# GpSimd in place of SyncE as the issuer of four loads and the first store in a one-core elementwise kernel

## The chip, the cores and the metric

The kernel runs on one core of a Trainium2 chip. The metric is the device time of one execution in microseconds; the median of three runs before the change is 119.82 us (119.6 to 119.83).

The core has several engines, each with its own queue of instructions. Here VectorE (DVE) multiplies, ScalarE (ACT) applies the activation, and SyncE (SP), ACT and GpSimd (POOL) may issue DMA transfers between HBM and the on-chip memory SBUF, which has 128 partitions. The transfers themselves are carried out by 16 DMA engines. TensorE (PE) does nothing in this kernel. Engines wait for each other through semaphores.

## The reference

Both inputs are float32 arrays of 1024 x 4096 elements, 16.8 MB each, and so is the output.

```python
z = x * y
return 0.5 * z * (1 + np.tanh(np.sqrt(2 / np.pi) * (z + 0.044715 * z ** 3)))
```

It is the product of x and y, put through the tanh form of GELU. Each element is read once from x and once from y, and written once: 33.55 MB in and 16.78 MB out.

## The kernel before, in words

The arrays are taken as flat and divided into three pieces, `PIECES`. Spread over 128 partitions, a piece has 1,280, 16,384 or 15,104 float32 columns; a row of it, the part of one partition, is contiguous in HBM and has 5,120, 65,536 or 60,416 bytes. I call them the small, the big and the last piece.

All of x has its place in SBUF (`xs`, 32,768 columns). The product and the activation overwrite it, and the stores read from there. For y there is only a buffer of 20,440 columns (`ys`), so the later y pieces reuse columns of the first one; `Y_LOADS` gives the order of the y pieces (big, last, small) and where each goes, and `Y_FREE` how many multiplications must be done before a load may overwrite.

The order of everything is written out by hand, with raw semaphores:

- `_hoist` puts two loads at the very start of the program: the small x piece on SP, and the big x piece on ACT.
- SP then waits for the small x piece, and issues the first y piece (big; `load_y`, L75) and the last x piece (`load_x`, L71). It waits until three multiplications are done and issues the second y piece (last), then until four are done and issues the third y piece (small).
- DVE multiplies (L99) in steps: four of 4,096 columns for the big piece, seven of 2,048 and one of 768 for the last piece, one of 1,280 for the small one. Each step raises `sem_mul`. Ahead of each piece DVE waits for its x and y.
- ACT applies GELU (L107) to the same columns after each multiplication and raises `sem_act`.
- SP issues the three stores, in the order big, last, small (L116), each when the activations of its piece are done (L115, L116). The first of them waits as well for `sem_y[-2]`, the landing of the second y piece. SP then waits for the first two stores (L118), clears the semaphores (L121) and waits for the last store (L122).

So five of the transfers that SP issues in the middle (four loads and the first store) stand in one queue with the stores that come after. The lines of the first store's waits are these:

```python
for i, (a, b) in enumerate(STORES):
    if i == 0:
        nc.sync.wait_ge(sem_y[-2], 16)
    nc.sync.wait_ge(sem_act, done[b])
```

Of the kernel before, what the change touches and what calls it, by code (L numbers as in the profile page):

```python
# [1 line left out]

# [4 lines left out]


F32 = mybir.dt.float32
GELU = mybir.ActivationFunctionType.Gelu_apprx_tanh  # L10

PIECES = [(0, 1280), (1280, 17664), (17664, 32768)]

Y_LOADS = [(1280, 17664, 4056), (17664, 32768, 0), (0, 1280, 15104)]

Y_FREE = [0, 3, 4]

STEPS = [[4096] * 4, [2048] * 7 + [768], [1280]]  # L20
STORES = [(1280, 17664), (17664, 32768), (0, 1280)]
Y_BUF = 20440


def _hoist(nc, issued):

    here = nc.cur_bb.bb.instructions
    first = nc.main_func.blocks[0].instructions
    for ins in issued:
        del here[next(k for k, i in enumerate(here) if i is ins or i.name == ins.name)]  # L30
    engine = issued[0].engine
    at = next(
        k
        for k, i in enumerate(first)
        if i.engine == engine and type(i).__name__ == "InstDrain"
    )
    first[at:at] = issued


@with_exitstack  # L40
def kernel(
    ctx: ExitStack,
    tc: tile.TileContext,
    x: bass.AP,
    y: bass.AP,
    out: bass.AP,
):
    nc = tc.nc
    P = nc.NUM_PARTITIONS

    def columns(t, a, b):

        flat = t.flatten_outer_dims().rearrange("r c -> (r c)")
        pa, pb = next(q for q in PIECES if q[0] <= a and b <= q[1])
        return flat[P * pa : P * pb].rearrange("(p c) -> p c", p=P)[:, a - pa : b - pa]


    tc.close()
    tc.compile()

    xs = nc.alloc_sbuf_tensor("xs", [P, PIECES[-1][1]], F32).ap()
    ys = nc.alloc_sbuf_tensor("ys", [P, Y_BUF], F32).ap()
    sem_x = [nc.alloc_semaphore(f"sem_x{i}") for i in range(len(PIECES))]
    sem_y = [nc.alloc_semaphore(f"sem_y{i}") for i in range(len(Y_LOADS))]
    sem_mul = nc.alloc_semaphore("sem_mul")
    sem_act = nc.alloc_semaphore("sem_act")
    sem_o = [nc.alloc_semaphore(f"sem_o{i}") for i in range(len(STORES))]

    def load_x(i, engine=nc.sync):
        a, b = PIECES[i]  # L70
        return engine.dma_start(out=xs[:, a:b], in_=columns(x, a, b)).then_inc(sem_x[i], 16)  # L71

    def load_y(i):
        a, b, r = Y_LOADS[i]
        return nc.sync.dma_start(  # L75
            out=ys[:, r : r + b - a], in_=columns(y, a, b)
        ).then_inc(sem_y[i], 16)

    _hoist(nc, [load_x(0).ins])
    _hoist(nc, [load_x(1, nc.scalar).ins])  # L80
    nc.sync.wait_ge(sem_x[0], 16)
    load_y(0)
    load_x(2)
    for i in range(1, len(Y_LOADS)):
        if Y_FREE[i]:
            nc.sync.wait_ge(sem_mul, Y_FREE[i])
        load_y(i)

    nc.scalar.wait_ge(sem_x[0], 16)
    n = 0  # L90
    done = {}
    for i, (a, b, r) in enumerate(Y_LOADS):
        for j, (xa, xb) in enumerate(PIECES):
            if xa <= a < xb:
                nc.vector.wait_ge(sem_x[j], 16)
        nc.vector.wait_ge(sem_y[i], 16)  # L96
        c = a
        for w in STEPS[i]:
            nc.vector.tensor_mul(  # L99
                out=xs[:, c : c + w],  # L100
                in0=xs[:, c : c + w],
                in1=ys[:, r + c - a : r + c - a + w],
            ).then_inc(sem_mul, 1)
            n += 1
            done[c + w] = n
            nc.scalar.wait_ge(sem_mul, n)
            nc.scalar.activation(  # L107
                out=xs[:, c : c + w], in_=xs[:, c : c + w], func=GELU
            ).then_inc(sem_act, 1)
            c += w  # L110

    for i, (a, b) in enumerate(STORES):
        if i == 0:
            nc.sync.wait_ge(sem_y[-2], 16)
        nc.sync.wait_ge(sem_act, done[b])  # L115
        nc.sync.dma_start(out=columns(out, a, b), in_=xs[:, a:b]).then_inc(sem_o[i], 16)  # L116
    for i in range(len(STORES) - 1):
        nc.sync.wait_ge(sem_o[i], 16)  # L118
    nums = sorted(s.num for s in [*sem_x, *sem_y, *sem_o[:-1], sem_mul, sem_act])
    assert nums == list(range(nums[0], nums[-1] + 1))  # L120
    nc.sync.sem_clear(range(nums[0], nums[-1] + 1))  # L121
    nc.sync.wait_ge(sem_o[-1], 16).then_inc(sem_o[-1], -16)  # L122


# [1 line left out]
_INS = ['x', 'y']  # L126
_OUTS = [((1024, 4096), 'float32')]


# [23 lines left out]
```

## Time and profile before

| | |
|---|---|
| median of the runs | 119.82 us (119.6 to 119.83) |
| span of the profiled execution, first to last instruction | 118.5 us |
| median less span: what lies around the instructions | 1.3 us |
| DVE busy | 35.2 us in 13 multiplications |
| ACT busy | 30.9 us, of it 29.6 in 13 activations |
| GpSimd busy | 0.2 us, four memsets at the start |
| moved by DMA | 50.33 MB, 425 GB/s on average over the span |
| DMA issues | 8 on SP, 1 on ACT |

The DMA issues of the profiled execution, with their times from the trace (issue to landing):

| transfer | issued by, at | landed after |
|---|---|---|
| small x, 640 KB | SP, 0.00 us | 13.6 us |
| big x, 8192 KB | ACT, 0.12 us | 30.4 us |
| first y (big) | SP, 13.57 us | 29.0 us |
| last x, 7552 KB | SP, 13.96 us | 46.5 us |
| second y (last) | SP, 55.79 us | 22.5 us |
| third y (small) | SP, 60.12 us | 19.7 us |
| first store (big) | SP, 78.27 us | 20.9 us |
| second store (last) | SP, 96.55 us | 20.4 us |
| third store (small) | SP, 97.71 us | 20.8 us |

A view of the page has one line per group or per queue. In the row of the DMA engines, each digit is the busy share of one fortieth of the span in tenths, over 16 engines. In the list of DMA queues the columns are packets, megabytes, and the share of 16 engines' span that the packets took. In the list of waits they are the total in microseconds, how often, and the longest. In the table of stretches they are the length, the busy time of DVE, ACT and GpSimd with the number of instructions, the granted TensorE clock, the DMA share and GB/s. "SPq" is SP's queue of instructions; q1 is the DMA queue that SP feeds, and q10 the one that ACT feeds.

### The profile page before, as it was taken

How to read it: one execution, taken by the hardware profiler on the slowest of the kernel's cores; microseconds unless marked ns; L12 is line 12 of the kernel's file. 1: busy time of each engine (PE TensorE's matmuls, PEld its weight loads, DVE VectorE, ACT ScalarE, POOL GpSimd, SP SyncE). 2: the span in 40 equal slices, each digit the busy share in tenths (PEclk: the TensorE clock that was granted, in tenths of full speed). 3: DMA queues.
4: the chain of work that ended last, by engine and by line, in shares of the span. 5: the costliest groups of instructions: out<-in, count | busy, mean ns of one | idle time of the engine just before them, and what ended most of it. 6: DMA issues, size and time to landing. Idle time of an engine off the chain costs nothing.

```text
span 118.5 us, 83 instructions
## 1 busy us (share of the span) xinstructions
DVE 35.2 (30%) x13; ACT 30.9 (26%) x14; POOL 0.2 (0%) x4
## 2 busy tenths in 40 slices
DVE  0000000000000069999920000059999940000000
ACT  0000000000000000999975000006998990000000
POOL 0000000000000000000000000000000000000000
DMA  9888899889988897798797797798899887977975
GB/s 492 382 382 382 354 597 464 354 354 465 597 354 354 354 632 347 326 632 347 326 632 347 326 632 347 326 575 354 354 531 531 354 354 326 653 326 326 653 326 221
DMA packets 1296, 50.33 MB, mean 425 GB/s; under 512 B 144, under 2 KB 144, under 8 KB 528
## 3 DMA queue, kind: packets, MB, share of 16 engines
q1 hardware_dynamic: 1152, 41.94, 82.3%
q10 hardware_dynamic: 144, 8.39, 16.5%
HBM read 33.55 MB, written 16.78 MB: 425 GB/s over the span
## 4 chain that ended last, share of the span: by engine, by line
DMA 55%; DVE 24%; ACT 3%; issue 1%; DVEq 0%
DMA ys<-in_y_dram 43%; DVE xs L99 24%; DMA xs<-in_x_dram 11%; ACT xs L107 3%; DVEq L96 0%
## 5 line engine op out<-in xcount | busy, mean ns | idle before, releaser
L99 DVE TENSOR_TENSOR xs<-xs,ys 128x2048 f32<-128x2048 f32 (+3 forms) x13 | 35.2, 2778 | 60.9 <-DMA ys<-in_y_dram 60.9
L107 ACT ACTIVATE xs<-xs 128x2048 f32<-128x2048 f32 (+3 forms) x13 | 29.6, 2300 | 19.6 <-DVE xs L99 19.6
L107 ACT ACT_TABLE_LOAD x1 | 1.3, 1283 | 47.2 <-DVE xs L99 47.2
L137 POOL MEMSET const-uint8-127<- 128x1 uint8 x1 | 0.1, 102 | 0.0
L137 POOL MEMSET const-bfloat16-1.0<- 128x1 bf16 x1 | 0.1, 101 | 0.0
L137 POOL MEMSET const-float32-0.0<- 128x1 f32 x1 | 0.1, 98 | 0.2 <-issue 0.2
L137 POOL MEMSET const-float32-1.0<- 128x1 f32 x1 | 0.1, 98 | 0.0
## 6 DMA issues: line engine op xcount, KB each, us to landing
xs<-in_x_dram SPq DMA_DIRECT2D x1, 7552.0 KB, 46.5
ys<-in_y_dram SPq DMA_DIRECT2D x1, 7552.0 KB, 22.5
out_dram<-xs SPq DMA_DIRECT2D x1, 7552.0 KB, 20.4
xs<-in_x_dram SPq DMA_DIRECT2D x1, 640.0 KB, 13.6
ys<-in_y_dram SPq DMA_DIRECT2D x1, 640.0 KB, 19.7
out_dram<-xs SPq DMA_DIRECT2D x1, 640.0 KB, 20.8
xs<-in_x_dram ACTq DMA_DIRECT2D x1, 30.4
ys<-in_y_dram SPq DMA_DIRECT2D x1, 29.0
```

Source lines behind the costliest of these rows:

```text
L99: nc.vector.tensor_mul(out=xs[:, c : c + w], in0=xs[:, c : c + w], in1=ys[:, r + c - a : r + c - a + w],).then_inc(sem_mul, 1)
L107: nc.scalar.activation(out=xs[:, c : c + w], in_=xs[:, c : c + w], func=GELU).then_inc(sem_act, 1)
L137: nc = _bacc.Bacc("TRN2", target_bir_lowering=False, num_devices=1)
```

## The change

GpSimd takes over the five transfers in the middle: the waits and the issues of all three y pieces, of the last x piece and of the first store. SP keeps the small x piece at the start, the second and third store and the waits at the end; ACT keeps the big x piece. The first store's wait for the second y piece is removed, and it waits for its activations alone. In GpSimd's queue the five stand in the order in which SP had them, after the memsets of the start.

```diff
     def load_y(i):
         a, b, r = Y_LOADS[i]
-        return nc.sync.dma_start(
+        return nc.gpsimd.dma_start(
             out=ys[:, r : r + b - a], in_=columns(y, a, b)
         ).then_inc(sem_y[i], 16)
 
     _hoist(nc, [load_x(0).ins])
     _hoist(nc, [load_x(1, nc.scalar).ins])
-    nc.sync.wait_ge(sem_x[0], 16)
+    nc.gpsimd.wait_ge(sem_x[0], 16)
     load_y(0)
-    load_x(2)
+    load_x(2, nc.gpsimd)
     for i in range(1, len(Y_LOADS)):
         if Y_FREE[i]:
-            nc.sync.wait_ge(sem_mul, Y_FREE[i])
+            nc.gpsimd.wait_ge(sem_mul, Y_FREE[i])
         load_y(i)
...
     for i, (a, b) in enumerate(STORES):
-        if i == 0:
-            nc.sync.wait_ge(sem_y[-2], 16)
-        nc.sync.wait_ge(sem_act, done[b])
-        nc.sync.dma_start(out=columns(out, a, b), in_=xs[:, a:b]).then_inc(sem_o[i], 16)
+        engine = nc.gpsimd if i == 0 else nc.sync
+        engine.wait_ge(sem_act, done[b])
+        engine.dma_start(out=columns(out, a, b), in_=xs[:, a:b]).then_inc(sem_o[i], 16)
```

## The prediction

> **What bounds the kernel now.** I read the page's DMA parts first, then the chain that ended last, the stretches of the span, the waits of SP's queue, and last the trace's records of single DMA packets.
>
> ```profile
> DMA  9888899889988897798797797798899887977975
> DMA packets 1296, 50.33 MB, mean 425 GB/s; under 512 B 144, under 2 KB 144, under 8 KB 528
> q1 hardware_dynamic: 1152, 41.94, 82.3%
> q10 hardware_dynamic: 144, 8.39, 16.5%
> ```
>
> SP's queue q1 and ACT's q10 together fill 98.8% of what 16 DMA engines have in 118.5 us, that is 117.1 us; only 1.4 us are empty. The packet records say where. The first packet starts at 1.01 us and the last ends at 118.13 us; in between 16 engines are busy nearly everywhere, one row of a piece per engine at a time. A row of 65,536 bytes takes 2.418 us, one of 60,416 bytes 2.229 us, one of 5,120 bytes 0.193 us from start to start. Two of these give a line, 4.45 ns a packet and 0.0368 ns a byte, and the third lies on it. Per engine 24 rows of each size make 116.2 us.
>
> ```profile
> 55.79 22.46 DMA ys<-in_y_dram
> ...
> 80.55 13.31 DVE xs L99 x6
> ```
>
> These are two pieces of the chain in order of time; in all DVE has 24% of it, which misleads here: the chain follows semaphores, and while DVE multiplies, the engines move other pieces.
>
> ```profile
> 42.60:55.80 13.20, 13.14 (x4) 8.41 (x4) 0.00 (x0) 1.00 1.01 439
> 55.80:60.50 4.70, 4.30 (x1) 3.98 (x2) 0.00 (x0) 1.00 0.95 411
> 60.50:78.30 17.80, 0.00 (x0) 3.25 (x1) 0.00 (x0) 1.00 0.93 401
> ```
>
> The column before the last is the DMA share (a packet counts where it starts, so short stretches wobble). It is about 1 with DVE busy for 13.14 of 13.20 us. So the time is bytes over 16 engines, plus whatever empties them. An edit can gain only what is empty now, and it loses whatever it empties.
>
> ```profile
> SPq L75 <- DVE xs L99: 45.4, 2, 41.4
> ...
> SPq L116 <- DMA ys<-in_y_dram: 14.5, 1, 14.5
> SPq L75 <- DMA xs<-in_x_dram: 12.1, 1, 12.1
> SPq L115 <- ACT xs L107: 3.3, 1, 3.3
> ```
>
> These are the waits that move to GpSimd, and the one that goes: the first store had its activations at 63.77 us (L115) and was held 14.5 us more until the second y piece landed.
>
> **The change, part by part.** The profiled span is 118.5 us and the median of the runs 119.82; I carry the 1.3 us between them unchanged. The trace of before has no DMA issued by GpSimd. What it costs from its wait's end to its first packet, L, I bound by the SP rows: 0.84 us (first store, 78.27 to 79.11) and 1.01 us (first x piece, 0.00 to 1.01) below, and by 3.82 us above (SP's first y piece, 13.57 to 17.39, though most of that is two of ACT's rows ahead of it). I take 1.5 us, nearest to the rows with nothing ahead; what counts is whether it stays under the cover at each place.
>
> The Trainium skill ("DMA: Bandwidth & Descriptors", section "Latency and other measured facts") gives about 1 us to the first byte from GpSimd and 0.6 us from SP; by that, as an estimate, L would be 1.4 us and the sum the same. No run here shows it yet.
>
> First y piece and last x piece: GpSimd waits for the first x piece (13.56 us) and has nothing else after its four memsets at 0.3 us. The cover is ACT's x piece: its fifth row of eight starts at 12.56 to 13.21 us, so four rows, 9.7 us, are still to move. If L were 8.7 us, the engines would just run dry. Each row less of y early is a row more of x: the first y piece still lands last, near 42.6. The x piece is behind it by 19 us. Cost 0.
>
> Second y piece: issued when three multiplications are done, 55.79 us. The last rows of x before it end at 59.38 to 60.07 us by engine (mean 59.68). Cover 3.6 us against L = 1.5: cost 0, up to 0.2 at L = 3.82, and 1 us for each us beyond. Third y piece: 60.11 us, with 17 us of rows ahead. Cost 0.
>
> First store: issued at 63.77 instead of 78.27 us, behind the second and third y pieces on the same queue. If GpSimd's queue keeps order as SP's does (the last x piece was issued 0.38 us after the first y piece, and its rows start only at 41.55, after all of y), the store's rows follow without a gap. What goes is the present gap: per engine, from the third y piece's last packet (78.74 to 79.44) to the store's first row (79.11 to 79.45), 0 to 0.36 us, mean 0.14. The latest engine has no gap, so the end gains between 0 and 0.14; I take 0.1.
>
> Other two stores: still SP's, at 96.55 and 97.7 us. They wait for ACT, which hangs on the second y piece, not on the store. Before, the first store's rows end at 98.53 to 98.77; SP's rows can be ready at 96.55 + 1.0 = 97.55. Cover 1.0 us, 0.9 when the store starts 0.1 earlier. Cost 0. If the y piece's landing were signalled over 0.9 us later than SP's (0.4 to 0.5 us after the last packet now), that would be paid. SP's last waits (L118 to L122) hang on the last store as before.
>
> Sum: 0 + 0 + 0 - 0.1 + 0 = -0.1 us: span 118.4, time 119.7, no change that can be measured (0.2%, 0.24 us, is about what a measurement of this kernel can tell; the runs shown spread by 0.23).
>
> **The rivals.**
>
> *DVE holds up GpSimd (slower).* The second y piece is issued 0.1 us after the fourth multiplication begins (55.68 to 60.10 us), which reads two operands from SBUF. If GpSimd could not prepare the transfer beside it, the first row would come at 60.10 + 1.5 = 61.6 (61.0 to 62.3) against 59.68: 1.9 us empty, time 121.6. It decides as soon as the hold passes 59.4 - 1.5 = 57.9 us. Nothing in the trace has GpSimd beside DVE, so nothing speaks against it; chance 0.12. The Trainium skill ("SBUF — State Buffer", section "Who interferes with whom") warns of GpSimd's descriptor writes being locked out by DVE's two-port modes, but excepts the two-input multiplication, which takes only the shared read side. By it this rival falls and the sum stands; the trace agrees only that the multiplication runs at one element a cycle or less (4,096 in 4.42 us).
>
> *Rows cut small (slower).* Before moves each row as one packet. If GpSimd's path cut them at 4,096 bytes, each engine would have 15, 14, 14 and 15 more packets a row for eight rows of the four large transfers, 464 packets of 4.45 ns: 2.1 us, time 121.8. The line through the three row sizes carries that price; nothing shows the cut. Chance 0.10.
>
> *One slow engine (slower).* Transfers end with their slowest engine. Before, every engine's rows agree within 1% in the loads from 15 us on; the slowest rows there are the first ones of the first store, 2.454 us (median), 36 ns over the loads'. If one engine had that on each of the 32 big rows that move to GpSimd, it ends 1.2 us late: 121.0. Chance 0.09. The skill's DMA page (same section) says that engines 7 and 15 are usually slower, as a best guess because of rings that GpSimd's transfers use; no run here shows it.
>
> *Breaks between transfers (slower).* On SP's queue the next transfer's row starts 6 to 15 ns after the last one's semaphore packet. If GpSimd's queue paused for 0.14 us, the gap now before the store, at its four boundaries: +0.56 - 0.1, time 120.3. Chance 0.06.
>
> *The store does not wait its turn (slower).* If GpSimd's queue served the store beside the second y piece from 65.5 us on, that piece's 5.4 rows left would alternate with rows of 2.42 us and land 13 us later; DVE and ACT then take their 18.2 us (78.34 to 96.53) behind the engines: 12 us empty before the second store, time 131.7. SP's order speaks against it. Chance 0.03.
>
> *Stores run smoother (faster).* The store rows now take 2.423 and 2.231 us on average from start to start, load rows 2.4165 and 2.2265; over 16 rows this is 0.09 us, and with the 36 ns of the first rows 0.11 at most. If both this and the whole gap of 0.14 went: -0.25, time 119.57. Nothing else in the middle is empty, so more than that needs time outside the packets. Chance 0.17; it stands for any gain past the bound.
>
> That the change does nothing at all is my forecast, nearly: the engines are full, and who fills them is all that differs.
>
> **How the numbers follow.** No change 0.43, the likeliest single case, its own range 119.6 to 119.95. Faster 0.17. Slower 0.12 + 0.10 + 0.09 + 0.06 + 0.03 = 0.40. The predicted time is 119.7. For the range I go down to 119.3 (the 0.25 us and as much again as runs differ) and up to 121.9, over the cut rows and most of the held second y piece; outside lie the misplaced store, longer holds and large gains, less than 2 in 10.
>
> **What would show it.** Right: a third queue with about 33 MB, its rows still one packet each at 2.42 and 2.23 us; all queues together at 98.8% or above; the second y piece landing near 78.2 us; the store's issue near 63.8 us, and its first rows within 0.05 us of the third y piece's last packets. Wrong: a dip of the DMA row near 60 us with rows starting after 60.1 (DVE's hold, or an L over 3.6 us); more packets than 1,296 (cut rows); engines that drift apart by more than the 0.7 us they have now; a y piece landing near 91 us (order lost). If the packets look the same and the time still differs, the 1.3 us around the span is where I was wrong.

## The result and the profile after

The changed kernel takes 121.71 us (median; 121.59 to 121.84) against 119.77 us beside it: ratio 1.0164, 95% interval 1.0149 to 1.0178. The change costs 1.9 us. The profiled execution of it took 121.83 us with a span of 120.5 us, so the 1.3 us around the span are as they were, and all of the loss is inside it.

The page after, its row of the DMA engines and the list of queues (packets, MB, share of 16 engines' span):

```profile
DMA  9888998899889978979979979598899889979975
...
DMA packets 1296, 50.33 MB, mean 418 GB/s; under 512 B 144, under 2 KB 144, under 8 KB 528
...
q0 software_dynamic: 720, 32.90, 64.4%
q1 hardware_dynamic: 432, 9.04, 17.8%
q10 hardware_dynamic: 144, 8.39, 16.2%
```

q0 is the queue that GpSimd feeds. The number of packets and their sizes are unchanged, so no row was cut; the three queues together still fill 98.4% of a longer span. The engines are hardly emptier than before. They are slower somewhere. The row of digits has a 5 in its middle, in the slice from 75.3 to 78.3 us; the row of before has none but at its end.

The waits of GpSimd's queue, where SP's stood before, and its issues in order of time:

```profile
POOL ys L75 <- DVE xs L99: 44.8, 2, 41.0
POOL ys L75 <- DMA xs<-in_x_dram: 13.2, 1, 13.2
POOL out_dram L115 <- ACT xs L107: 3.1, 1, 3.1
```

```profile
13.68 0.67 POOL L75 DMA_DIRECT2D ys<-in_y_dram  x1 [13.24 <-DMA xs<-in_x_dram]
14.34 0.53 POOL L71 DMA_DIRECT2D xs<-in_x_dram  x1
...
55.87 0.53 POOL L75 DMA_DIRECT2D ys<-in_y_dram  x1 [41.00 <-DVE xs L99]
...
60.21 0.53 POOL L75 DMA_DIRECT2D ys<-in_y_dram  x1 [3.81 <-DVE xs L99]
63.85 0.54 POOL L115 DMA_DIRECT2D out_dram<-xs  x1 [3.12 <-ACT xs L107]
```

The issues come where the prediction had them. The one at 55.87 us runs beside a DVE multiplication (55.5 to 59.9 us) and the one at 60.21 beside none; both take 0.53 us, and so DVE does not hold GpSimd up. This is what the Trainium skill ("SBUF — State Buffer", section "Who interferes with whom") excepts from its warning, and here the trace agrees.

The table of stretches shows the place (length, busy DVE, ACT, GpSimd, clock, DMA share, GB/s). First before, then after:

```profile
75.00:82.00 7.00, 3.66 (x2) 1.33 (x1) 0.00 (x0) 1.00 1.22 523
```

```profile
75.00:82.00 7.00, 3.26 (x2) 0.93 (x1) 0.00 (x0) 1.00 1.06 364
```

A packet's bytes count where it starts. 523 less 364 GB/s in 7 us is 1.11 MB: a round of store rows (16 of 65,536 bytes) has moved past 82 us. In the same view cut to 74 to 82 us, each slice is 0.2 us, and the small y rows can be seen. First before, then after:

```profile
GB/s 0 0 0 0 302 1812 1812 604 302 0 0 0 0 0 0 0 154 333 410 435 410 410 410 384 231 3681 1336 328 0 0 0 0 0 0 0 0 0 2294 2621 328
```

```profile
GB/s 0 0 0 0 604 1510 1510 906 0 302 0 0 0 0 0 0 0 26 51 128 102 282 128 179 230 230 179 205 205 333 384 1920 1162 1715 681 26 26 328 0 0
```

The burst at about 75 us is the last big y rows, the long low stretch is the small y rows (640 KB), and the next burst is the store's first rows. Before, the small rows run at some 410 GB/s for 1.6 us. After, they run mostly at 100 to 230 GB/s for about 2.6 us, and begin late. In the packet records, the last big y row takes 2.79 us (median) instead of 2.23, a small row up to 0.74 instead of 0.196, and the store's first rows start at 80.61 us on average instead of 79.19. So 1.4 us are lost between 75 and 81 us. Besides, the engines have drifted apart: their first store rows start between 80.25 and 81.47 us (79.11 to 79.45 before), so the latest engine is already 2.0 us behind here. The last engine ends at 120.15 us (118.13 before), the same 2.0 us.

The second store's first row, the first on SP's queue behind GpSimd's, lasts 2.52 us from start to start on average (2.24 before). The view of DMA from 98 to 106 us, in slices of 0.2 us, shows which engines pay for that: its first burst is the start of this row, its second burst the start of the next.

```profile
GB/s 0 328 0 0 0 0 0 604 906 1510 1208 302 0 302 0 0 0 0 0 0 906 1812 302 1208 302 302 0 0 0 0 0 604 2115 302 906 604 302 0 0 0
```

The burst reaches from 99.4 to 100.8 us and the next from 102.0 to 103.2: the early engines need 2.6 us and more, the last one 2.2. In the packet records seven engines, all of them starting before 99.9 us, have a row of 2.43 to 3.19 us, one has 2.28, and the eight that start later have the usual 2.23. So in this execution the engine that ends last loses nothing at the second store.

### The profile page after: what moved, and what is told of

It is laid out like the page before. It is cut to its first block, busy times and chain, and to the rows that moved or that the text cites. A ratio compares the mean times of both kernels' runs of the same rounds, so it can differ in the third digit from the quotient of the medians.

```text
span 120.5 us, 82 instructions
## 1 busy us (share of the span) xinstructions
DVE 35.2 (29%) x13; ACT 30.9 (26%) x14; POOL 3.0 (2%) x9
## 2 busy tenths in 40 slices
DMA packets 1296, 50.33 MB, mean 418 GB/s; under 512 B 144, under 2 KB 144, under 8 KB 528
## 4 chain that ended last, share of the span: by engine, by line
DMA 54%; DVE 23%; ACT 3%; issue 2%; DVEq 0%
DMA ys<-in_y_dram 43%; DVE xs L99 23%; DMA xs<-in_x_dram 11%; ACT xs L107 3%; DVEq L96 0%
## 5 line engine op out<-in xcount | busy, mean ns | idle before, releaser
L75 POOL DMA_DIRECT2D ys<-in_y_dram x3 | 1.7, 574 | 58.0 <-DVE xs L99 44.8
L115 POOL DMA_DIRECT2D out_dram<-xs x1 | 0.5, 536 | 3.1 <-ACT xs L107 3.1
L71 POOL DMA_DIRECT2D xs<-in_x_dram x1 | 0.5, 528 | 0.0
```

What stands on the lines that cost most here:

```text
L75: return nc.gpsimd.dma_start(out=ys[:, r : r + b - a], in_=columns(y, a, b)).then_inc(sem_y[i], 16)
L115: engine.dma_start(out=columns(out, a, b), in_=xs[:, a:b]).then_inc(sem_o[i], 16)
```

## The experiments

Two theories came out of this. **Q**: a store that stands in the queue right behind loads slows the last of these loads, whoever issues it; here the removed wait is what costs. **G**: GpSimd's own transfers are slow, and the wait was of no use. The first four runs separate the removed wait from the change of issuer.

**SP without the wait.** Before, less two lines:

```diff
-        if i == 0:
-            nc.sync.wait_ge(sem_y[-2], 16)
```

> SP issues everything as before, only the first store's wait for the second y piece is gone. Theory Q (the store queued right behind the loads slows the last loads, whoever issues it): the last row of the second y piece takes about 2.8 us instead of 2.23 and the small y rows about 0.32 us instead of 0.196, 1.4 us lost between 75 and 81 us, time 121.2. Theory G (GpSimd's own transfers are slow or break at their boundaries, the wait is harmless): rows as before, the gap of 0.14 us ahead of the store closes, time 119.7.

Measured: 120.97 us, ratio 1.0092 (1.0074 to 1.0110). The last big y row takes 2.90 us, the small rows after it 1.9 us instead of 1.6, and the store starts at 80.54 us. Of the 1.35 us that this is later than before, 0.5 were there when the last big row began (75.79 us against 75.27), and 0.3 already at 60 us, ahead of the store's issue; they are of this execution and are not shown to be the store's. From the start of the last big row to the store's first row it is 4.75 us, against 3.92 before and 5.36 in the changed kernel. So the loss is there with SP as the issuer, in this trace smaller (0.8 us) than with GpSimd (1.4 us). GpSimd issues no transfer here. The landings (us after issue) of the second and third y piece, 22.5 and 19.7 before, show it on the page:

```profile
ys<-in_y_dram SPq DMA_DIRECT2D x1, 7552.0 KB, 23.5
...
ys<-in_y_dram SPq DMA_DIRECT2D x1, 640.0 KB, 20.9
```

**After, with the wait kept on GpSimd.**

```diff
+        if i == 0:
+            engine.wait_ge(sem_y[-2], 16)
         engine.wait_ge(sem_act, done[b])
```

> As after, but GpSimd's first store keeps the wait for the second y piece. Theory Q: the last y rows are at 2.23 and 0.196 us again; a gap of some 0.3 us ahead of the store (GpSimd's issue is slower than SP's), and the 0.3 us where the second store's queue takes over may stay: time 119.9 to 120.3. Theory G: as after, 121.7.

Measured: 121.53 us, ratio 1.0137 (1.0121 to 1.0152). That fits neither theory: the time lies above what Q allowed, and the rows are not slow as G wants them. The last y rows are clean (2.23 us), as Q wants, but the time did not come back. The packet records show two new losses: the store's first rows start at 80.01 us on average, a gap of 0.8 us, and the second store's first row takes 3.04 us in every engine, 0.8 us too long.

**GpSimd loads, SP stores.** All three stores are SP's, the first with its wait, as before; the four loads are GpSimd's, as after.

> GpSimd issues the four loads, SP all three stores, the first with its wait for the second y piece. Theory Q: 119.8, as before. Theory G: the last y rows are slow although no store is queued behind them, 121.2 or more.

Measured: 119.86 us, ratio 0.9999 (0.9990 to 1.0009). Its page:

```profile
ys<-in_y_dram POOLq DMA_DIRECT2D x1, 7552.0 KB, 22.2
...
ys<-in_y_dram POOLq DMA_DIRECT2D x1, 640.0 KB, 19.4
```

The time is that of before and all four loads are GpSimd's. G falls: four of the five moved transfers cost nothing.

**SP loads, GpSimd issues only the first store**, with its wait.

> SP issues the loads, GpSimd only the first store, with its wait for the second y piece. Theory Q: 119.8 to 120.2, the excess being GpSimd's later issue and the change of queue behind the first store (0.3 us in after). Theory G: no load is GpSimd's, so the loads run as before; the same 119.8 to 120.2, unless the store's own transfer breaks.

Measured: 121.43 us, ratio 1.0125 (1.0108 to 1.0142), far over what I expected. The loads are clean; the gap and the slow first row of the second store are there as in the run before last (first rows at 79.92 us; 3.05 us). So the store's issuer has a price of its own, even with the wait. I formed a third theory, **H**: the change of queue between two stores costs 0.8 us.

**All stores on GpSimd**, with and without the wait. SP waits for all three and clears the semaphores last.

```diff
-        engine = nc.gpsimd if i == 0 else nc.sync
+        engine = nc.gpsimd
+        if i == 0:
+            engine.wait_ge(sem_y[-2], 16)
```

> GpSimd issues the four loads and all three stores, the first with its wait for the second y piece; SP waits for all stores and clears the semaphores last. Theory H (the change from GpSimd's queue to SP's between the first and second store costs 0.8 us: the second store's first row took 3.05 us instead of 2.25): that row is at 2.25 again, only the 0.8 us gap ahead of the first store is left, time 120.6. Rival (a store on GpSimd's queue costs that at its end, whoever comes next): the row stays at 3 us, time 121.5.

> The same without the first store's wait. Theories Q and H together: the last y rows are slow as with SP without the wait (1.1 to 1.4 us lost by 81 us), no loss at the second store: 121.0. Rival (the wait's loss and the queue's loss have one cause, a store on GpSimd's queue): 121.7 as after.

Measured: 120.40 us, ratio 1.0054 (1.0039 to 1.0069), and 121.15 us, ratio 1.0117 (1.0101 to 1.0132). With the stores in one queue the second store's first row is back at 2.27 and 2.23 us. Without the wait the loss of 1.4 us by 81 us remains (the store starts at 80.57), and the end is 0.7 us earlier than in the changed kernel. With the wait, GpSimd's slower issue is left: 0.28 us from the landing to its start and 1.1 us on to the first packet. The changed end has a share in both times: here the span ends 0.5 us after the last packet, in the other kernels 0.4.

**The first store on ACT's queue**, with its wait, behind ACT's four activations of the big piece.

> Before, but the first store is issued by ACT, after its four activations of the big piece, with the same wait for the second y piece; second and third store on SP. Theory H for any two queues: no gap ahead of the first store, but the second store's first row takes 3 us: 120.6. Rival (only GpSimd's queue has this at its end): 119.9.

Measured: 120.67 us, ratio 1.0078 (1.0061 to 1.0095). Here GpSimd issues nothing, and the second store's first row takes 3.06 us. The view of DMA from 95 to 103 us, in slices of 0.2 us, has a burst at each round of rows. First before, then this run:

```profile
GB/s 0 0 0 0 0 4588 655 0 0 0 0 0 0 0 0 0 0 2719 2115 0 0 0 0 0 0 0 0 0 1510 3323 0 0 0 0 0 0 0 0 0 302
```

```profile
GB/s 0 0 0 0 1638 3277 328 0 0 0 0 0 0 0 0 0 0 4531 302 0 0 0 0 0 0 0 0 0 0 0 0 604 2719 1510 0 0 0 0 0 0
```

The first burst is the first store's last round, the second the second store's first. From there to the next it is about 11 slices before and 15 here. H holds for ACT's queue as for GpSimd's. In these runs all 16 engines pay (rows of 2.90 to 3.32 us), but in the changed kernel only those pay that came to the second store before 99.9 us, within 2.9 us of its issue at 96.95. So a change of queue does not always cost this. Whether the second store would be free if it were issued earlier was not tried.

**The third store later.** In both kinds of run SP's issue of the third store lasts 2.0 to 2.8 us instead of 0.33, which might be a cause. In this run SP waits for the first store's landing before it.

> The first store on ACT's queue as in the run before it, and SP's third store waits until the first one has landed, so that only the second store follows the change of queue. Theory H: the second store's first row still takes 3 us, time 120.6. Rival (it is the third store's issue, 2.5 to 2.8 us long there instead of 0.33, that disturbs the row): 2.25 us, 119.9.

Measured, in one execution: 120.63 us; the second store's first row takes 3.06 us still, and the third store's issue 0.56 us. So the length of that issue is not the cause. The issue itself, at 99.01 us, now falls into the row's time, and so this run does not exclude that some issue there matters.

**A load in place of the store.** SP without the wait; the first store is replaced:

```diff
+        if i == 0:
+            nc.sync.dma_start(out=xs[:, a:b], in_=columns(x, a, b)).then_inc(sem_o[0], 16)
+            continue
```

> SP without the wait, and in place of the first store a load of the big x piece again into the same columns of SBUF (the big piece of the output is not written). Theory D (what slows the last loads is that a store stands behind them): the last y rows are at 2.23 and 0.196 us, no loss, time 119.6 to 119.8. Rival B (any third transfer queued behind the two does it): 2.9 and 0.32 us, 121.0.

Measured, in one execution: 119.83 us. The y pieces land after 22.5 and 19.7 us, as before, and the rows are at 2.23 and 0.196 us. The same number of bytes in the same place of the queue, but as a load, cost nothing. Of the two, only the store slows the loads ahead of it.

**How early is too early?** ACT, idle from 63.8 to 80.7 us, works on unused columns of `ys`, and SP's store waits for that in place of the second y piece (`sem_d` counts those activations):

```diff
-            nc.sync.wait_ge(sem_y[-2], 16)
+            nc.sync.wait_ge(sem_d, 4)
```

The second of the two runs has two activations in place of four, and waits for 2.

> Before, but the first store is issued by time and not by the second y piece's landing: ACT, idle then, does four activations on unused columns of ys (extra work, no part of the result), and SP issues the store when they are done, near 77.2 us instead of 78.27, while the engines move the small y rows. Theory T (the store costs the loads only if it stands in the queue before an engine begins its last big load row, from 75.0 on): rows stay at 2.23 and 0.196 us, the gap of 0.14 us closes, 119.7. Rival (any store ahead of the loads' end slows what is left of them): part of the 1.3 us, 120.2 or more.

> The same with two such activations: the store issued near 71.1 us, three big rows ahead of the small ones. Theory T: the whole loss of the version without the wait, last y row 2.8 to 2.9 us, 121.0 to 121.2. Rival (the loss grows with the time that the store stands in the queue, 14 us there and 7 here): half of it, 120.4.

Measured: issued at 76.92 us, 119.85 us, ratio 1.0008 (0.9999 to 1.0017); issued at 70.88 us, 121.06 us in one execution. At 70.88 the whole loss is there (the store starts at 80.36 us), although the store stands in the queue for seven microseconds less than without the wait. At 76.92 the rows are clean and the store follows the small rows without a gap. The limit lies between the two runs and is not narrowed further. The start of the last big y row (75.0 to 75.7 us), which I had expected it to be, is there; so is the start of the small rows (77.3 to 77.9 us), if the 0.84 us from SP's issue to the first packet are added to 76.92.

The same view as above, 74 to 82 us, of the run issued at 70.88:

```profile
GB/s 0 0 0 0 0 1208 1812 1510 302 0 0 0 0 0 0 0 0 128 128 154 256 230 154 282 256 179 128 333 205 307 1265 2197 1992 328 0 0 0 0 0 0
```

The last big row runs nearly as usual (2.34 us, where I had expected 2.8 to 2.9) and almost the whole loss is in the small rows.

**Without the small y piece.** SP without the wait, the third y piece not loaded.

> SP without the wait, and the small y piece isn't loaded (its multiplication takes what lies in ys, so the small piece of the output is not the product asked for). Theory S (the loss needs the small rows between the last big load row and the store): last big y row 2.23 us, the store's rows follow at once; with 640 KB or 1.55 us less to move, the time is 118.2. Rival (a store right behind big load rows slows them as well): last row 2.8 us or more, 118.8 to 119.5.

Measured, in one execution: 120.28 us. The last big y row takes 3.26 us, and the store's row comes 3.30 us after its start instead of 2.23: 1.1 us lost with no small row in between. The small rows are not needed for it. Two more losses bring the time over the range: the last big row begins 0.6 us later than before (75.84 us against 75.27), for which I have no cause, and a gap of 0.55 us stands ahead of the second store, whose activations now come too late.

## Why the prediction was wrong

The predicted time was 119.7, no change; it is 121.71, slower. That it still lies within the stated range of 119.3 to 121.9 is luck: the range went so high for cut rows and for a second y piece held up by DVE, and neither happened. Of the signs named beforehand, one of the wrong ones came: the engines drifted apart by 1.2 us at the first store. Step by step:

- What bounds the kernel: right. The DMA engines are the bound, rows keep their sizes, and DVE's place in the chain does not matter. (The 2.418 and 2.229 us of a row are the packet's duration; from start to start it is 2.4165 and 2.2265. Nothing hangs on the difference.)
- First y piece, last x piece, second and third y piece at cost 0: right, shown by the run with GpSimd's loads and SP's stores (0.9999). L was taken as 1.5 us; measured are 0.28 to 0.30 us from the wait's end to the instruction and 1.1 us on to the first packet, 1.4 in all, where nothing lies ahead of it. That is the estimate made from the Trainium skill's figure ("DMA: Bandwidth & Descriptors", section "Latency and other measured facts"). All four covers held.
- First store, "the store's rows follow without a gap", worth 0 to -0.14: this step failed. The order was kept and the gap did close, but the last load rows paid 1.4 us for the store behind them. I priced the removed wait by the gap that it leaves, and took a queued transfer to be free until its turn. No row of the trace of before has a store queued behind more than its last small rows, which should have been a reason for a bound on the other side.
- "Other two stores: cost 0", because their issue is covered: failed as well, though its share of the time is open. The issue is covered, but the second store now stands in another queue than the first. That costs 0.8 us where the engines arrive together. In the changed kernel it costs seven engines 0.2 to 1.0 us and the engine that ends last nothing.
- The sum by the runs: with all stores on GpSimd and no wait, the store behind loads costs 1.4 us (121.15 against 119.74). The changed kernel is some 0.6 us slower than that (121.71 against 121.15; the two were timed beside different runs of before, 119.77 and 119.74). That these 0.6 us are the change of queue is argued and not shown. The trace of the changed kernel has them on its last engine ahead of the first store (81.47 us, against 80.79 with all stores on GpSimd), where the two kernels are still the same, so there they belong to the execution. The engines that did pay at the second store reach their next row by 102.84 us, against 102.34 for the latest with all stores on GpSimd. My estimate from these two is that they would end the kernel some 0.5 us later even where no engine drifts.
- The rivals: DVE's hold, cut rows, one slow engine and breaks between transfers fall, by the 0.53 us issues, the 1,296 packets, and the clean run of GpSimd's loads. One row of the changed kernel, at 59 to 62 us, did take 2.71 us, but the last big y row begins at 75.26 us on average, as before (75.27). The rival that came nearest was the store that disturbs the second y piece, but its mechanism, the store's rows served in turn with the loads' at a cost of 12 us, was not what happened: its rows came after all loads.
- The rival "stores run smoother": the run issued at 76.92 us closes the gap and its store rows run at 2.418 us, and it gains nothing (1.0008, 0.9999 to 1.0017). The last engine ended at 118.09 us, against 118.13: as the prediction said, the latest engine had no gap to lose.

What happens inside a DMA engine is open. The runs show when it occurs (a store issued at 70.88 us or earlier, behind loads whose last rows end at 79.4 us in the kernel before; two consecutive stores in different queues, if the engine comes to the second within 2.9 us of its issue) and when not (a load there; a store issued 0.8 to 2.2 us ahead of its turn; loads in different queues; all stores in one queue), and not the cause. No version tried beats the kernel before.

## What to carry to other kernels

A wait ahead of a store may be there for its timing and not for its data: before taking it out, ask what stands in the same queue ahead of the store, and try the removal by itself. Where the DMA engines are full, as here, keep consecutive stores in one queue, and try the first store's issue while the last loads are under way: here 76.92 and 78.27 us took the same time, and an issue at 70.88 us or at once, when the data was ready, cost 1.1 to 1.4 us. Who issued the loads did not matter here, where each issue had other transfers to cover it.

## What the runs showed that I had not expected

A store queued behind loads costs 1.1 to 1.4 us of time once, at the end of these loads, and no more when it is queued 15 us ahead (120.97 us) than 8 (121.06 us); a load there costs nothing. A store that follows another store in a different queue starts with a row of 3.05 us instead of 2.25 where it comes to its turn 2.0 to 2.9 us after its issue, with ACT's queue as with GpSimd's; in the changed kernel the engines that came to it later than that did not pay. A store that follows loads in a different queue does not (2.45 us for 65,536 bytes, in the run with GpSimd's loads, as before).
